# A Griffin-style residual block: eight instead of six of the eleven inner tiles of the last projection as block products

## The chip, the cores and the metric

The kernel runs on one core of a Trainium2 chip. The metric is the device time of one execution in microseconds (us); three runs of the kernel before gave a median of 869.18 us (869.02 to 870.11). The engines of the core are called PE (TensorE, matrix products), DVE (VectorE), ACT (ScalarE), POOL (GpSimd) and SP (SyncE, which here only issues transfers). PE writes its sums to PSUM, eight banks of 128 x 512 floats; everything else lies in SBUF.

## The reference

One trunk layer on 512 frames of 1024 features: an RMS norm, one wide projection, banded attention and an RG-LRU branch, a gated merge, and then the part that the change is about:

```python
h = h + (g_a * ya + g_b * yb) @ w_o[l]
hn = rmsnorm(h, norm_ffn_g[l])
gu = hn @ w_ffn_in[l]                       # 1024 x 5632
g, up = jnp.split(gu, 2, axis=-1)
h = h + (jax.nn.silu(g) * up) @ w_ffn_out[l]   # 512 x 2816 times 2816 x 1024
return rmsnorm(h, final_norm_g)
```

All is float32. A product in this kernel is three matmuls: every operand is split into a high part (type fp32r) and a low remainder, and high x high, high x low and low x high are summed (`mm3`, lines 76 to 78). A split is one ACT copy (the high part, line 82) and then one DVE subtraction (the low part, line 83).

## The kernel before, in words

The stages run one after the other: norm and projections with the RG-LRU work; `v` and the product `yb` with the RG-LRU output (at 160 to 234 us of the profile); attention, head by head; the product `ya` with the attention output (432 to 479 us); `po_h` with `w_o`; norm; the wide feed-forward projection; and the last projection (from 753 us). The order of instructions on each engine and the slots of the buffers come from a planner that simulates the kernel. Inside `manual_schedule(engines={PE, DVE})` the order on PE and on DVE is the order of the program text; ACT's and SP's order is still the planner's. A buffer belongs to a tag with a fixed number of slots, and a new tile waits until all users of the tile that held its slot are done.

**The last projection** has 2816 inner rows, eleven inner tiles of 256. The activations of inner tile i are `act2[i]`, 128 x 2 x 512 floats. The output is eight quarters (t, cc), four token tiles of 128 by two column halves of 512; each has a PSUM bank (`quarter`). A *plain tile* of one inner tile on one quarter is 6 matmuls of 512 columns (`plain_tile`), 48 for all eight quarters.

Two inner tiles together form a *unit*, which is multiplied by the Winograd form of Strassen's scheme: the activations of a unit are four blocks a11, a12, a21, a22 (`part_of`; two inner tiles by two token halves), its weights four blocks b11, b12, b21, b22, and seven block products take the place of eight: a11 x b11, a12 x b21, s1 x t1, s2 x t2, s3 x t3, s4 x b22, a22 x t4, where

```
s1 = a21 + a22    s2 = s1 - a11    s3 = a11 - a21    s4 = a12 - s2
```

and t1 to t4 are such sums of the weights. The weight sums are made far earlier by `spill`: four loads of 512 KB, four DVE subtractions of 128 x 1024, four stores to DRAM (`sums_d`). Every block product is 12 matmuls per unit, in one half of the tokens and one column half (`multiply`). All units add up in PSUM, and between products DVE adds a bank's sum to the rows of `h` that need it (`read`, and `add` for the plain sums).

`make(a, b)` prepares a product: for each unit it loads the weight block (`fo_part`, line 928), splits it into `whl` (128 x 1024 on ACT and DVE), then splits the activation block into `x_` (`act_part`, 128 x 512). The slots: seven for the raw loads, ten for `whl`, and **eight for `x_` (tag "act" of pool `op`)**, which the high and low parts of some plain tiles share. `act2`, the sums and the other plain parts share the 13 slots of the tag "act" of pool `acp`.

Before, the inner tiles are `front` 0, 1, 2 (plain), units (3,4), (5,6), (7,8), and `tail` 9, 10 (plain, at the end, token tile by token tile). The sums s1, s2, s3 of all units are made in one block of DVE work, `act_sums`, while the plain tiles run; s4 in `act_last_sum`. In the tail, each token tile is finished as soon as its two quarters are complete: add to `h` (line 969), sum of squares on ACT (line 971), product with the norm's weights (line 972), then `h_norm`: root, reciprocal, scaling, and the stores.

## Time and profile before

| | |
|---|---|
| median of the runs | 869.18 us |
| the profiled execution, its own time | 869.43 us |
| its span in the trace | 867.6 us |
| PE busy | 855.7 us (99%) |
| DVE busy | 593.1 us (68%) |
| ACT busy | 495.0 us (57%) |
| POOL busy | 96.8 us (11%) |
| moved by DMA | 107.38 MB, 124 GB/s on the mean |

The span is the time between the first and the last event of the trace; some 1.8 us of the execution lie outside. A busy PE means that matmuls are in flight; their ends are modelled, so the distance between starts tells more than busy time does. In a row of a timeline the columns are the start in us, the duration, the engine, the line, the operation, the tile written and those read, and the shape; in brackets stands the idle time of the engine before the instruction and what ended it.

### The profile page before, as it was taken

The page shows a single profiled execution, that of the slowest core. Times are in us where ns is not written, and L with a number is a line of the kernel's source. Part 1 is how long each engine was busy: PE and PEld are TensorE (multiplying, and loading weights), DVE is VectorE, ACT ScalarE, POOL GpSimd, SP SyncE. Part 2 cuts the span into 40 slices and gives each one's busy share as a digit, 9 for nine tenths or more (in the row PEclk, how much of TensorE's full clock was granted, in tenths as well). Part 3 has the DMA queues.
Part 4 walks back from the last instruction along what each step waited for, and adds up shares of the span by engine and source line. Part 5 has one row for each costly group of instructions (what it writes and reads, how often), then busy time and mean ns, then how long its engine had stood idle before and what let it go on. Part 6 is the DMA issues. An engine that isn't in the chain of part 4 may idle for free.

```text
span 867.6 us, 12923 instructions
## 1 busy us (share of the span) xinstructions
PE 855.7 (99%) x4938; PEld 750.3 (86%) x4938; DVE 593.1 (68%) x914; ACT 495.0 (57%) x854; POOL 96.8 (11%) x135
## 2 busy tenths in 40 slices
PE   8999999999999999999999999999999999999996
PEld 6977887888888888888888889999999999888885
DVE  5787776676556656566556556888878888498554
ACT  7588687542366656577633365646555555456504
POOL 2022212110112313222200000000000001000001
PEclk9999999999999999999999999999999999999999
DMA  8222324589542213232223721433433333375402
GB/s 271 91 88 90 97 82 129 199 294 363 149 126 68 73 54 105 73 116 68 72 77 120 266 67 32 150 94 102 142 97 98 98 98 120 124 246 167 145 1 97
DMA packets 89934, 107.38 MB, mean 124 GB/s; under 512 B 5904, under 2 KB 71040, under 8 KB 89872
## 3 DMA queue, kind: packets, MB, share of 16 engines
q1 hardware_dynamic: 86192, 98.89, 35.7%
q10 hardware_dynamic: 3680, 7.67, 2.8%
q8 instruction: 39, 0.64, 0.3%
q14 instruction: 23, 0.19, 0.1%
HBM read 98.11 MB, written 8.43 MB: 123 GB/s over the span
## 4 chain that ended last, share of the span: by engine, by line
PE 86%; DVE 5%; ACT 5%; issue 2%; DMA 2%; POOL 0%; SPq 0%; ACTq 0%; POOLq 0%; DVEq 0%
PE po_out L76 4%; PE po_out L78 4%; PE po_out L77 4%; PE p_fg L76 2%; PE o L711 2%; PE p_fu L78 2%; PE p_fg L78 2%; PE p_fu L77 2%; PE p_fg L77 2%; PE p_fu L76 2%; PE pT L691 2%; PE po_ga L76 2%; PE po_ga L78 2%; PE po_ya L76 2%; PE po_h L78 2%
## 5 line engine op out<-in xcount | busy, mean ns | idle before, releaser
L680 POOL TENSOR_SCALAR p<-p,rl 128x128 f32<-128x128 f32 (+1 forms) x64 | 39.6, 637 | 160.6 <-DVE rl L678 160.5
L677 ACT ACTIVATE p<-p,m 128x128 f32<-128x128 f32 (+1 forms) x64 | 35.8, 562 | 13.2 <-DVE m L676 13.2
L917 POOL TENSOR_TENSOR act_lo<-act,act_hi 128x1024 fp32r<-128x1024 f32 x1 | 2.4, 2417 | 298.6 <-ACT act_hi L916 298.6
L83 DVE TENSOR_TENSOR pp<-pT,pp 128x384 fp32r<-128x384 f32 (+1 forms) x48 | 27.8, 596 | 9.8 <-ACT pp L82 9.7
L83 DVE TENSOR_TENSOR whl_qk<-raw_qk,whl_qk 128x1024 fp32r<-128x1024 f32 x16 | 21.5, 1345 | 14.4 <-ACT whl_qk L82 14.4
L76 PE MATMUL po_out<-whl_fo,act_hi 128*128 128x512 f32 (+1 forms) x80 | 30.8, 385 | 0.5 <-ACT c_u L283 0.5
L78 PE MATMUL po_out<-whl_fo,act_lo 128*128 128x512 f32 (+1 forms) x80 | 30.7, 384 | 0.0
L77 PE MATMUL po_out<-whl_fo,act_hi 128*128 128x512 f32 (+1 forms) x80 | 30.7, 384 | 0.0
L676 DVE CUSTOM_DVE_ANT_0 p<-s,bias 128x128 f32<-128x128 f32 (+1 forms) x64 | 29.2, 483 | 1.8 <-PE s L673 1.8
L83 DVE TENSOR_TENSOR whl_fg_s<-s_fg,whl_fg_s 128x1024 fp32r<-128x1024 f32 x20 | 25.6, 1291 | 5.0 <-ACT whl_fg_s L82 5.0
L76 PE MATMUL po_gr<-xnT,whl_gr 128*128 128x512 f32 (+1 forms) x80 | 28.1, 352 | 0.1
L77 PE MATMUL po_xr<-xnT,whl_xr 128*128 128x512 f32 (+1 forms) x80 | 27.9, 354 | 0.0
L77 PE MATMUL po_gr<-xnT,whl_gr 128*128 128x512 f32 (+1 forms) x80 | 27.8, 348 | 0.0
L78 PE MATMUL po_gr<-xnT,whl_gr 128*128 128x512 f32 (+1 forms) x80 | 27.5, 348 | 0.0
L83 DVE TENSOR_TENSOR whl_fu_s<-s_fu,whl_fu_s 128x1024 fp32r<-128x1024 f32 x20 | 24.0, 1222 | 5.2 <-ACT whl_fu_s L82 5.2
L78 PE MATMUL po_xr<-xnT,whl_xr 128*128 128x512 f32 (+1 forms) x80 | 27.3, 346 | 0.0
L76 PE MATMUL po_xr<-xnT,whl_xr 128*128 128x512 f32 (+1 forms) x80 | 26.6, 351 | 0.6 <-ACT xnT L363 0.6
L82 ACT ACTIVATE whl_fg_s<-s_fg 128x1024 fp32r<-128x1024 f32 x20 | 20.9, 1054 | 10.4 <-PE q_fg L78 5.5
L82 ACT ACTIVATE whl_qk<-raw_qk 128x1024 fp32r<-128x1024 f32 x16 | 16.8, 1051 | 16.2 <-PE po_yb L78 8.8
L76 PE MATMUL po_gb<-xnT,whl_gb 128*128 128x512 f32 x64 | 25.2, 393 | 0.3 <-DVE sp_p L455 0.3
L76 PE MATMUL po_ga<-xnT,whl_ga 128*128 128x512 f32 x64 | 25.3, 395 | 0.0
L77 PE MATMUL po_gb<-xnT,whl_gb 128*128 128x512 f32 x64 | 25.3, 395 | 0.0
(387 smaller groups left out, 3188.0 us busy)
## 6 DMA issues: line engine op xcount, KB each, us to landing
raw_fg<-in_w_ffn_in_dram SPq DMA_DIRECT2D x24, 512.0 KB, 4.4
raw_fu<-in_w_ffn_in_dram SPq DMA_DIRECT2D x22, 512.0 KB, 3.7
raw_qk<-in_w_in_dram SPq DMA_DIRECT2D x32, 256.0 KB, 3.2
spill<-in_w_ffn_out_dram SPq DMA_DIRECT2D x12, 512.0 KB, 4.7
sums<-spill SPq DMA_DIRECT2D x12, 512.0 KB, 3.7
raw_t<-sums SPq DMA_DIRECT2D x12, 512.0 KB, 4.5
raw_fo<-in_w_ffn_out_dram SPq DMA_DIRECT2D x10, 512.0 KB, 4.6
raw_b<-in_w_ffn_out_dram SPq DMA_DIRECT2D x9, 512.0 KB, 4.4
```

The source lines that it names most:

```text
L76: pe.matmul(o, sh, mh, start=start, stop=False, skip_group_check=parts)
L77: pe.matmul(o, sh, ml, start=False, stop=False, skip_group_check=parts)
L78: pe.matmul(o, sl, mh, start=False, stop=stop, skip_group_check=parts)
L82: act.activation(hi, src, AF.Copy)
L83: dve.tensor_sub(lo, src, f(hi))
L676: dve.tensor_tensor_reduce(prob[qb][:], scs[qb], bias[:, S - w:S], -1.0, 3e38, ALU.add, ALU.min, nmax[:, qb:qb + 1])
L677: act.activation(prob[qb][:], prob[qb][:], AF.Exp, bias=nmax[:, qb:qb + 1], scale=-1.0, accum_out=lsum[:, qb:qb + 1])
L680: pool.tensor_scalar(prob[qb][:], prob[qb][:], rl[:, qb:qb + 1], 1.0, ALU.mult, ALU.mult)
L691: pe.transpose(pt[:, at * P:(at + 1) * P], prob[qb][:, kb * P:(kb + 1) * P], ident[:])
L711: pe.matmul(po[:, S - n:S], st, pp[i][:, part, lo:lo + n], start=kb == 0 and part == 0, stop=kb == NT - 1 and part == 1)
L917: (pool if i == 0 else dve).tensor_sub(lo[:], o[:], f(hi[:]))
```

## The change

`front` becomes 0, 1, 10, the units are (2,3), (4,5), (6,7), (8,9), and there is no tail: eight inner tiles go through block products, three stay plain, all three ahead. Four things go with it:

- The sums s1 to s4 are made one at a time, each right before the split that needs it (`act_sum`, called in `act_part`), and s2, s3 and s4 in place.
- The weight sums of the fourth unit need a fourth `spill`. Spill 0 stays where it is; spill 1 moves from the first to the third step of `yb`; spills 2 and 3 are now made in `ya`, at steps 0 and 4, in slots that held queries and keys.
- The order of the products changes, and a12 x b21 comes first, onto the plain sums of quarters (0,0) and (1,0).
- The last two products on the second token half go tokens by tokens: all units for one token tile, then all units for the next. The last unit of the last one is cut into two column halves of 256. `finish` takes the place of `h_out`.

```diff
-    front, units, tail = (0, 1, 2), ((3, 4), (5, 6), (7, 8)), (9, 10)
+    front, units = (0, 1, 10), ((2, 3), (4, 5), (6, 7), (8, 9))
...
-    SPILLS = (0, 3)
     for j in range(KT):
...
-        if j in SPILLS:
-            spill(SPILLS.index(j) + 1)
+        if j == 2:
+            spill(1, [(aw2, "pt", 4)] * 4)
...
     for j in range(KT):
+        if j in (0, 4):
+            spill(2 + j // 4, [(aw, "qk", 3), (qkp, "qk", 3)] * 2)
         py = mm_tile(f"po_ya{j}")
...
-        pl, bufs = (op, 8) if i in front[1:] else (acp, 13)
+        pl, bufs = (op, 8) if i == 1 else (acp, 13)
...
     def act_part(name, u):
-        src = sum_of_act[name, u] if name[0] == "s" else part_of(name, u)
+        src = act_sum(name, u) if name[0] == "s" else part_of(name, u)
         o = op.tile([P, 2, 2, 256], F32R, tag="act", bufs=8, name=f"x_{name}{u}")
         split_pair(o, src)
...
+    def act_sum(name, u):
+
+        if name == "s1":
+            if u % 2 == 0:
+                s_tiles.append(acp.tile([P, 2, 2, 256], F32, tag="act", bufs=13, name=f"s_{u}"))
+            o = s_tiles[-1][:, u % 2]
+            dve.tensor_add(o, part_of("a21", u), part_of("a22", u))
+        elif name == "s2":
+            o = s_tiles[u // 2][:, u % 2]
+            dve.tensor_sub(o, o, part_of("a11", u))
...
+    def finish(cc, t, po, eng, i, at, added=False):
+
+        hs = ht[t][:, cc * S + at.start:cc * S + at.stop]
+        if not added:
+            dve.tensor_add(hs, po[:, at], hs)
+        junk = op.tile([P, S], F32, tag="junk", bufs=2, name=f"oj{t}_{i}")
+        act.activation(junk[:, at], hs, AF.Square, accum_out=osq[t][:, i:i + 1])
+        eng.tensor_mul(hs, hs, g_fin[:, cc * S + at.start:cc * S + at.stop])
...
+        for i, before in zip(front, (None, 1, 10)):
+            if before:
+                split_act(before)
+                for cc in range(2):
+                    fo_plain(before, cc)
+            if i == front[-1]:
+                make("a12", "b21")
+                make("a11", "b11")
+            for t, cc in ((2, 0), (3, 0), (0, 1), (1, 1), (2, 1), (3, 1), (0, 0), (1, 0)):
+                plain_tile(i, t, cc, i == 0)
         make("s1", "t1")
-        for t, cc in ((2, 0), (3, 0), (0, 1), (1, 1), (3, 1)):
+        for t, cc in ((2, 0), (3, 0), (0, 1), (1, 1), (2, 1), (3, 1)):
             add(t, cc)
+        multiply("a12", "b21", 0, 0, False)
         make("s2", "t2")
         multiply("a11", "b11", 1, 0, True)
         read(1, 0, (0, 0))
         multiply("s1", "t1", 0, 1, True)
-        make("a12", "b21")
+        make("s4", "b22")
         read(0, 1, (1, 1))
-        for u in every_unit:
-            act_last_sum(u)
         multiply("s2", "t2", 1, 0, False)
         make("s3", "t3")
         read(1, 0, (0, 1))
...
+        multiply("s4", "b22", 0, 1, False)
         make("a22", "t4")
...
+        for t in range(2):
+            finish(0, t, quarter[t, 0], pool, 0, every)
+        multiply("s3", "t3", 1, 0, False, (0,))
+        multiply("s3", "t3", 1, 0, False, (1,))
+        read(1, 0, (1, 1), (0,))
+        for t in range(2):
+            part = out_norm(t, 1)
+            finish(1, t, quarter[t, 1], dve, 1, every)
+            h_norm(t, part, 1)
+        finish(1, 2, None, pool, 0, every, True)
+        multiply("a22", "t4", 1, 0, False, (0,))
+        read(1, 0, (1, 1), (1,))
+        finish(1, 3, None, pool, 0, every, True)
+        most, last = range(len(units) - 1), [len(units) - 1]
+        multiply("a22", "t4", 1, 0, False, (1,), most)
+        for at in (slice(0, CW), slice(CW, S)):
+            multiply("a22", "t4", 1, 0, False, (1,), last, at)
...
```

More of the change, by code (lines that the diff above doesn't have):

```diff
@@ L741, in fo_block, with spill @@
         return rows.rearrange("(k p) e -> p k e", p=P)
-    def spill(u):
-        r = [aw2.tile([P, 2, S], F32, tag="pt", bufs=4, name=f"spill{u}_{n}") for n in range(4)]
+    def spill(u, rooms):
+        r = [pl.tile([P, 2, S], F32, tag=tag, bufs=bufs, name=f"spill{u}_{n}") for n, (pl, tag, bufs) in enumerate(rooms)]
         for n in range(4):
@@ L754, in spill @@
             sp.dma_start(out=sums_d[u][n][:], in_=r[i][:])
-    spill(0)
+    spill(0, [(aw2, "pt", 4)] * 4)
     for t in range(NT):
         v_tile(0, t)
-    SPILLS = (0, 3)
     for j in range(KT):
@@ L963, in block_kernel @@
     osq = [cp.tile([P, 4], F32, name=f"osq{t}") for t in range(NT)]
-    def h_out(cc, t, po, eng, i, at):
-        n = slice(cc * S + at.start, cc * S + at.stop)
-        hs = ht[t][:, n]
-        dve.tensor_add(hs, po[:, 0:at.stop - at.start], hs)
-        junk = op.tile([P, S], F32, tag="junk", bufs=2, name=f"oj{t}_{i}")
-        act.activation(junk[:, 0:at.stop - at.start], hs, AF.Square, accum_out=osq[t][:, i:i + 1])
-        eng.tensor_mul(hs, hs, g_fin[:, n])
     def out_norm(t, parts):
@@ L1014, in part_of @@
         return act2[units[u][tile_]][:, :, half * 256:half * 256 + 256]
-    sum_of_act = {}
     def act_part(name, u):
-        src = sum_of_act[name, u] if name[0] == "s" else part_of(name, u)
+        src = act_sum(name, u) if name[0] == "s" else part_of(name, u)
         o = op.tile([P, 2, 2, 256], F32R, tag="act", bufs=8, name=f"x_{name}{u}")
@@ L1022, in act_part @@
         acts[name, u] = o
-    def act_sums(u):
-        t = acp.tile([P, 2, 2, 256], F32, tag="act", bufs=13, name=f"s12_{u}")
-        s1, s2 = t[:, 0], t[:, 1]
-        a11, a21, a22 = (part_of(n, u) for n in ("a11", "a21", "a22"))
-        dve.tensor_add(s1, a21, a22)
-        dve.tensor_sub(s2, s1, a11)
-        dve.tensor_sub(a21, a11, a21)
-        sum_of_act.update({("s1", u): s1, ("s2", u): s2, ("s3", u): a21})
-    def act_last_sum(u):
-        a12 = part_of("a12", u)
-        dve.tensor_sub(a12, a12, sum_of_act["s2", u])
-        sum_of_act["s4", u] = a12
+    def act_sum(name, u):
[7 more added lines that the diff above has]
+            dve.tensor_sub(o, o, part_of("a11", u))
+        elif name == "s3":
+            o = part_of("a21", u)
+            dve.tensor_sub(o, part_of("a11", u), o)
+        else:
+            o = part_of("a12", u)
+            dve.tensor_sub(o, o, s_tiles[u // 2][:, u % 2])
+        return o
+    s_tiles = []
     of_weights = {"b11": (0, 0), "b21": (1, 0), "b22": (1, 1)}
@@ L1045, in make, with multiply @@
             act_part(a, u)
-    def multiply(a, b, half, cc, start):
-        for u in range(len(units)):
-            for i in range(2):
+    def multiply(a, b, half, cc, start, tokens=range(2), us=None, at=every):
+        for u in us or range(len(units)):
+            for i in tokens:
                 x, w = acts[a, u], parts_w[b, u]
@@ L1052, in multiply @@
                 for k in range(2):
-                    mm3(quarter[2 * half + i, cc][:], x[:, 0, k, tok], x[:, 1, k, tok], w[:, 0, k], w[:, 1, k],
+                    mm3(quarter[2 * half + i, cc][:, at], x[:, 0, k, tok], x[:, 1, k, tok], w[:, 0, k, at], w[:, 1, k, at],
                         start and u == 0 and k == 0, u == len(units) - 1 and k == 1, parts=True)
-    def read(half, cc, into=None):
-        for i in range(2):
-            t, to = 2 * half + i, 2 * (half if into is None else into[0]) + i
-            n = cc if into is None else into[1]
-            hs = ht[to][:, n * S:(n + 1) * S]
-            dve.tensor_add(hs, quarter[t, cc][:], hs)
@@ L1064, in block_kernel, with read @@
-    every_unit = range(len(units))
-    everywhere = [(t, cc) for cc in range(2) for t in range(NT)]
-    with tc.manual_schedule(engines={mybir.EngineType.PE, mybir.EngineType.DVE}):
-        split_act(1)
-        fo_plain(1, 0)
-        fo_plain(1, 1)
-        for t, cc in everywhere:
-            plain_tile(front[0], t, cc, True)
-        split_act(2)
-        fo_plain(2, 0)
-        fo_plain(2, 1)
-        for t, cc in everywhere:
-            plain_tile(front[1], t, cc, False)
-        make("a11", "b11")
-        for u in every_unit:
-            act_sums(u)
-        for t, cc in ((2, 0), (3, 0), (0, 1), (1, 1), (3, 1), (0, 0), (1, 0), (2, 1)):
-            plain_tile(front[2], t, cc, False)
+    def read(half, cc, into, tokens=range(2)):
+        for i in tokens:
+            hs = ht[2 * into[0] + i][:, into[1] * S:(into[1] + 1) * S]
+            dve.tensor_add(hs, quarter[2 * half + i, cc][:], hs)
@@ L1088, in block_kernel @@
         multiply("s1", "t1", 0, 1, True)
-        make("a12", "b21")
+        make("s4", "b22")
         read(0, 1, (1, 1))
-        for u in every_unit:
-            act_last_sum(u)
         multiply("s2", "t2", 1, 0, False)
@@ L1095, in block_kernel @@
         read(1, 0, (0, 1))
-        multiply("a12", "b21", 0, 0, False)
-        make("s4", "b22")
-        multiply("s3", "t3", 1, 0, False)
-        read(1, 0, (1, 1))
+        multiply("s4", "b22", 0, 1, False)
         make("a22", "t4")
-        multiply("s4", "b22", 0, 1, False)
-        for i in tail:
-            split_act(i)
-            for cc in range(2):
-                fo_plain(i, cc)
-        multiply("a22", "t4", 1, 0, False)
-        for t in range(NT):
-            for i in tail:
-                plain_tile(i, t, 0, False)
-            h_out(0, t, quarter[t, 0], pool, 0, every)
-            pieces = [(quarter[t, 1], every, False)]
-            if t == NT - 1:
-                last = mm_tile("po_last")
-                pieces = [(quarter[t, 1], slice(0, CW), True), (last, slice(CW, S), True)]
-            for n, (po, at, start) in enumerate(pieces):
-                for i in tail:
-                    plain_tile(i, t, 1, start and i == tail[0], at, po[:, 0:at.stop - at.start])
-                if n == len(pieces) - 1:
-                    part = out_norm(t, n + 1)
-                h_out(1, t, po, dve, n + 1, at)
-            h_norm(t, part, n + 1)
+        for t in range(2):
[15 more added lines that the diff above has]
+            multiply("a22", "t4", 1, 0, False, (1,), last, at)
+        part = out_norm(2, 1)
+        finish(0, 2, quarter[2, 0], dve, 1, every)
+        h_norm(2, part, 1)
+        finish(0, 3, quarter[3, 0], dve, 1, slice(0, CW))
+        part = out_norm(3, 2)
+        finish(0, 3, quarter[3, 0], dve, 2, slice(CW, S))
+        h_norm(3, part, 2)
 _INS = ["x", "norm_mix_g", "w_in", "b_merge", "rel_table", "w_attn_out", "conv_w", "conv_b", "w_rg_r", "b_rg_r",
```

## The prediction

> **What bounds the kernel now.** I read the page's engine line first, then PE's waits, then the busy time by stage.

> ```profile
> span 867.6 us, 12923 instructions
> PE 855.7 (99%) x4938; PEld 750.3 (86%) x4938; DVE 593.1 (68%) x914; ACT 495.0 (57%) x854; POOL 96.8 (11%) x135
> ...
> PE po_out L76 <- ACT c_u L283: 0.5, 1, 0.5
> ...
> PE po_v L76 <- DVE v L83: 0.3, 1, 0.3
> ...
> 753.00:782.00 29.00, 28.81 (x127) 23.85 (x128) 27.05 (x33) 18.40 (x23) 0.00 (x0) 1.00 0.73 251
> 782.00:839.00 57.00, 57.00 (x253) 47.20 (x252) 40.39 (x48) 25.62 (x32) 0.00 (x0) 1.00 0.36 113
> 839.00:861.00 22.00, 22.00 (x109) 18.59 (x107) 9.79 (x21) 9.60 (x23) 4.99 (x4) 1.00 0.19 72
> ```

> The last three rows are the last projection: plain tiles, products, tail. Their columns are the stretch, busy time (and count) of PE, weight load, DVE, ACT and POOL, the granted clock, DMA share and GB/s. PE waits there once, 0.5 us. DVE is busy 40.4 of 57 us beside the products and 9.8 of 22 in the tail: it follows PE with room, and the change spends that room.

> ```profile
> 753.19 0.50 PE L76 MATMUL po_out<-whl_fo,act_hi 128*128 128x512 f32 x1 [0.47 <-ACT c_u L283]
> ...
> 830.86 0.39 PE L76 MATMUL po_out<-whl_t,x_a 128*128 128x512 f32 x1
> ...
> 838.79 0.39 PE L78 MATMUL po_out<-whl_t,x_a 128*128 128x512 f32 x1
> ...
> 859.37 0.28 PE L78 MATMUL po_out<-whl_fo,act_lo 128*128 128x256 f32 x1
> ...
> 859.49 0.28 PE L76 MATMUL po_last<-whl_fo,act_hi 128*128 128x256 f32 x1
> ...
> 859.69 0.42 DVE L969 TENSOR_TENSOR h<-po_out,h 128x256 f32<-128x256 f32 x1 [0.65 <-PE po_out L78]
> ...
> 860.81 0.28 PE L78 MATMUL po_last<-whl_fo,act_lo 128*128 128x256 f32 x1
> ```

> The 36 matmuls of a22 x t4 start from 830.86 to 838.79: 7.93 / 35 = 0.2266 us each. So 6 of them (a unit on one token tile, or a plain tile on a quarter) take 1.36 us, a unit in a product 2.72, a product of four units 10.88. The twelve half-width ones from 859.49 to 860.81 stand 0.12 apart; PE is through at 860.93.

> **PE's work.** Before, 5 x 48 + 3 x 7 x 12 = 492 matmuls, twelve of them cut into 24 halves: 480 x 0.2266 + 24 x 0.12 = 111.65 us. After, 3 x 48 + 4 x 7 x 12 = 480, six of them cut into twelve halves: 474 x 0.2266 + 12 x 0.12 = 108.85. **PE saves 2.8 us.**

> **DVE's work in a product.** Rows of DVE and ACT while s1 and t1 are prepared:

> ```profile
> 768.29 0.69 DVE L1028 TENSOR_TENSOR s<-act,act 128x512 f32<-128x512 f32 x1
> ...
> 769.01 0.63 ACT L82 ACTIVATE x_s<-s 128x512 fp32r<-128x512 f32 x1 [0.28 <-DVE s L1028]
> ...
> 774.08 1.22 DVE L83 TENSOR_TENSOR whl_t<-raw_t,whl_t 128x1024 fp32r<-128x1024 f32 x1
> 775.22 0.69 DVE L83 TENSOR_TENSOR x_s<-s,x_s 128x512 fp32r<-128x512 f32 x1
> 775.82 1.22 DVE L83 TENSOR_TENSOR whl_t<-raw_t,whl_t 128x1024 fp32r<-128x1024 f32 x1
> ```

> Back to back, DVE needs 1.14 us for a unit's weights and 0.60 for its `x_`: 1.74. In the new order the sum comes between them, and `x_` needs ACT's copy of that very sum: 1.14 + sum 0.69 + 0.04 + ACT 0.63 + 0.04 + 0.60 = **3.14 us per unit** (0.04 is the hand-over: 768.29 + 0.69 to 769.01). Four units make 12.56, and two `read` adds 1.2 more: 13.76 us of DVE for each of s1, s2, s4, s3, against 10.88 of PE. Before, the sums were made ahead and DVE never stood between them and the split. So DVE becomes the bound, if it has no lead.

> **Its lead is cut by the slots.** `x_` has eight slots. These rows show such slots at work before: the copy waits for the PE product that last used its slot, and one `x_` follows the other at 2.72 us, PE's time for a unit.

> ```profile
> 787.54 0.63 ACT L82 ACTIVATE x_a<-act 128x512 fp32r<-128x512 f32 x1 [1.14 <-PE po_out L78]
> ...
> 790.26 0.63 ACT L82 ACTIVATE x_a<-act 128x512 fp32r<-128x512 f32 x1 [1.14 <-PE po_out L78]
> ...
> 821.54 0.69 DVE L1062 TENSOR_TENSOR h<-po_out,h 128x512 f32<-128x512 f32 x1 [9.00 <-PE po_out L78]
> ```

> The third row is the other half of it: DVE stood 9 us at a `read`, in program order, with later work behind it. After the change, a12 and a11 of four units fill all eight slots. `x_` of s1, unit u, waits until PE is through with a12, unit u. In DVE's text the six `add`s stand behind all of s1, and PE's next product a11 x b11 overwrites quarters (2,0), (3,0), so it waits for the first `add`. Queued there: a11 on PE, and behind the adds all of s2.

> The chain, with PE never late until then: 753.19 + 126 plain matmuls (18 of 144 ran earlier, inside the feed-forward) x 0.2266 = 781.75, a12 begins. Unit 0 is done at 784.5, drained 0.16 later (0.39 - 0.23); ACT and DVE make s1's first `x_` by 785.95. Three more units at 3.14: 795.4. First add 0.69: **a11 starts at 796.1; PE was free at 792.6, so it stalls 3.5 us.** All adds end at 799.0; s2 and reads 812.8; s4 and reads 826.5; s3 839.1 and the first read 839.8. PE could start s3 x t3 at 796.1 + 43.5 = 839.6: stall 0.2. Second read 840.3, a22 (4 x 1.74) 847.3, two finishing adds 1.2, the first read of s3 0.6: 849.1. Then DVE finishes tokens 0 and 1 ahead of the read that a22's second token tile needs. Their prices in the tail of before:

> ```profile
> 844.66 0.69 DVE L969 TENSOR_TENSOR h<-po_out,h 128x512 f32<-128x512 f32 x1 [1.08 <-PE po_out L78]
> ...
> 846.13 1.28 ACT L986 ACT_TABLE_LOAD   x1
> ...
> 848.49 0.68 DVE L969 TENSOR_TENSOR h<-po_out,h 128x512 f32<-128x512 f32 x1
> ...
> 850.10 0.69 DVE L969 TENSOR_TENSOR h<-po_out,h 128x512 f32<-128x512 f32 x1
> ...
> 852.92 0.69 DVE L969 TENSOR_TENSOR h<-po_out,h 128x512 f32<-128x512 f32 x1
> ```

> 3.83 us for the first (844.66 to 848.49, with ACT's table load of 1.28) and 2.82 for the second (850.10 to 852.92): 855.75, the read 0.7: 856.5. PE has a22's first token tiles done at 839.8 + 16.3 = 856.1: stall 0.4. Then 18 matmuls and 12 halves, 5.5 us: PE ends at 862.0, **1.1 later than before**, though it has 2.8 less to do.

> **The end.** Before, the half that ends at 859.37 + 0.12 = 859.49 starts the last chain (add 859.69, square, product, add of the other half), 8.1 us to the end of the span; twelve half matmuls hide behind it. After, six do, so the first half is ready only 0.72 before PE's end where it was 1.44: **+0.7.** The sum so far is +1.8.

> **ACT in the way.** The 3.14 hold when ACT is free at the moment the sum is done, 16 times. ACT also copies the weights, 1.05 us each, in an order that the planner sets:

> ```profile
> L82 ACT ACTIVATE whl_t<-raw_t 128x1024 fp32r<-128x1024 f32 x12 | 12.3, 1048 | 8.1 <-issue 6.5 <-PE po_out L78 1.6
> ```

> No such meeting is to be seen before, since DVE had a lead. Bounds: 0, and a full copy in every second case, 8 x 1.05 = 8.4. I take chance (1.05 of 3.14, a third) times half a copy, 16 x 0.17 = 2.7, since nothing ties ACT's order to DVE's. All of it lies on the chain. **Sum: +4.5.**

> **The moved spills.** Four loads, four subtractions (about 1.2 us each like the other 128x1024 rows), four stores, on SP ahead of `ya`'s and `w_o`'s weight loads.

> ```profile
> 160.00:195.00 35.00, 34.70 (x156) 28.57 (x155) 24.07 (x31) 14.41 (x24) 6.47 (x4) 1.00 0.88 298
> ...
> 432.00:479.00 47.00, 47.00 (x211) 38.99 (x211) 28.94 (x36) 17.36 (x22) 0.00 (x0) 1.00 0.36 114
> ```

> `ya` has 18 us of free DVE for 10 us of subtractions, and two thirds of the DMA time for 8.4 MB. In the first row, where a spill and more shared the queue, PE lost 0.3 us. I take +0.3 here; bounds -0.3 (yb is relieved) and +2 (SP held at a store while `w_o` waits). The order of plain tiles changes which bank is first, so the 0.47 us ahead of 753.19 may go or double: 0, bounds +-0.5. `a22`'s and `s3`'s token-by-token order costs nothing: by then the chain on DVE, above, is late anyway. Tokens 2 and 3 have a product with the norm's weights on POOL, with products of PE ahead of its use.

> [...]

> ```profile
> 861.00:862.00 1.00, 0.09 (x1) 0.00 (x0) 0.97 (x4) 0.00 (x0) 0.18 (x1) 1.00 0.00 0
> ...
> 864.00:865.00 1.00, 0.00 (x0) 0.00 (x0) 0.00 (x0) 0.00 (x0) 0.00 (x0) 0.58 0.29 118
> ...
> 1.18 5.01 PE L309 MATMUL busy<-idle 128*128 128x512 bf16 x16 [1.18 <-DVE eps_t L315]
> ```

> PE ends at 861.09, and the granted clock falls to a half at 864.16 (0.58 is the mean of 0.16 at 1.00 and 0.84 at 0.50), 3.1 us later; a stall of 3.5 reaches that. The nearest price of a slow start is the 16 matmuls at the kernel's start, 5.01 us where 16 x 0.2266 are 3.63: 1.4. PE would then come to s3 at 841.0 and DVE at 839.8, and a22's wait would vanish: end 862.8 for 862.0 without ACT's waits, and nothing with them, since DVE then stays later than PE. [...]

> **Rivals.**
> - *PE still sets the time* (chance 0.13): the adds come through before PE needs them and ACT serves each sum at once, so only -2.8 + 0.7 = -2.1 remain: 867.3. For it: PE 99% busy, DVE with 17 us of room in the products before. Against: the count of eight slots and the text order leave s1's last `x_` no earlier than a12's end.
> - *DVE late, but little* (0.10): the stall at a11 is its minimum, 0.16 + 0.63 + 0.69 + 0.69 = 2.2, since DVE caught up on unit 3, and later stalls vanish: -2.8 + 2.2 + 0.7 = +0.1, 869.5. Against: 3.14 per unit is slower than the slots come free (2.72).
> - *SP blocks in `ya`* (0.05): a store waits for DVE, `w_o` behind it; one such hold, 4 subtractions of 1.2 us, +5 on whatever else holds, 879.
> - *The sums are not late in fact* (within the second): if s1 were ready before 781.75, ACT would still wait for the slot; the cycle would be 1.74 and the time that of the second rival.

> **How the numbers follow.** The profiled run took 869.43 us, 0.25 above the median. 869.43 + 4.5 + 0.3 = 874.2, against the median 873.9; this is the likeliest case (0.72). Its own range: without ACT's waits and spill 871.0; with 3 us more of ACT's waits and 1 of the spill 878. 0.2% is 1.7 us, about what a measurement of this kernel can tell from no change. Faster 0.13 (first rival), within 0.10 (second), slower 0.77. The range 869.4 to 878 leaves out the first rival and the far end of the third.

> **What would show it.** Right: a PE wait of 3 to 5 us for an `add`, at the first matmul of a11 x b11 some 39 us into the stage; DVE busy or waiting for ACT's `x_s` from there to s3; PE's matmuls 12 fewer; smaller waits at s3 and at a22's second token tile; the end 0.7 longer behind PE. Wrong: no PE wait at a11 (slots or order are not as I count), DVE's cycle far from 3.14, or idle PE in `ya` or `po_h`.

## The result, and the profile after

The changed kernel takes **884.66 us** (median, 883.74 to 885.75) where the kernel before takes 869.1 beside it: a ratio of 1.0177, with a 95% interval of 1.016 to 1.0195. That is 15.5 us slower. The forecast was 873.9, in a range of 869.4 to 878.0: the direction held, the size was three times too small. The profiled execution took 885.43 us, with a span of 883.6, which is 16.0 more than before.

The page of the changed kernel, its head, and from the list of costliest groups POOL's normalization of the attention's probabilities (busy time, then mean ns of one):

```profile
span 883.6 us, 12951 instructions
...
PE 859.6 (97%) x4920; PEld 751.1 (85%) x4920; DVE 605.9 (69%) x929; ACT 501.0 (57%) x862; POOL 102.1 (12%) x135
...
L680 POOL TENSOR_SCALAR p<-p,rl 128x128 f32<-128x128 f32 (+1 forms) x64 | 43.9, 703 | 163.8 <-DVE rl L678 163.7
```

PE has 18 matmuls less, and it waits more. Its waits, with the total, how often, and the longest:

```profile
PE pT L691 <- POOL p L680: 4.8, 4, 2.1
...
PE po_out L76 <- DVE h L999: 3.9, 1, 3.9
PE po_out L76 <- DVE h L1056: 1.7, 1, 1.7
...
PE po_out L76 <- DVE part L973: 0.9, 1, 0.9
PE po_out L77 <- DVE whl_fo L83: 0.8, 1, 0.8
```

The forecast named the second, third and fourth (line numbers of the changed kernel: 999 is the `add`, 1056 the `read`, 973 the norm of a token tile). It did not name the first, and that one is not in the last projection at all: line 680 normalizes the probabilities of an attention head, line 691 transposes them.

**Where the 16 us are.** PE's first plain product starts at 744.13 in the kernel before and at 751.58 after: 7.45 us are lost before the last projection begins. PE ends at 861.09 before and at 876.24 after: another 7.7 are lost inside it. The end of the span is 6.51 behind PE before, 7.36 after: the last 0.85.

**The attention's part.** Twenty microseconds around the last head. Columns as in the tables by stage: stretch, busy time (and count) of PE, weight load, DVE, ACT, POOL, granted clock, DMA share, GB/s. First the kernel before, then the changed one with stretches of 1 us below it:

```profile
420.00:440.00 20.00, 20.00 (x100) 16.96 (x99) 8.28 (x14) 8.07 (x16) 2.05 (x4) 1.00 0.20 60
```

```profile
420.00:440.00 20.00, 15.19 (x63) 12.21 (x62) 11.11 (x15) 6.15 (x12) 6.30 (x4) 0.83 0.74 263
...
427.00:428.00 1.00, 0.29 (x1) 0.14 (x1) 1.00 (x3) 0.00 (x0) 1.00 (x2) 0.92 0.98 389
428.00:429.00 1.00, 0.10 (x1) 0.00 (x0) 1.00 (x1) 0.00 (x0) 1.00 (x1) 0.50 1.20 272
...
434.00:435.00 1.00, 1.00 (x5) 0.83 (x4) 0.00 (x0) 0.00 (x0) 0.00 (x0) 0.67 0.79 313
```

POOL's four normalizations of the last head take 6.30 us instead of 2.05, PE stands idle for 4.8, and then the granted clock is at a half until some time in the stretch from 434. What stands beside POOL is DVE with the weight sums of the moved spills (lines 749 to 752), and the four normalizations apart show when it hurts. Rows of the changed kernel's timeline, then its groups of POOL by shape, then those of the kernel before:

```profile
422.46 1.22 DVE L749 TENSOR_TENSOR spill<-spill,spill 128x1024 f32<-128x1024 f32 x1 [0.91 <-DMA spill<-in_w_ffn_out_dram]
423.60 0.17 DVE L678 RECIPROCAL rl<-l 128x4 f32<-128x4 f32 x1
423.72 1.22 DVE L750 TENSOR_TENSOR spill<-spill,spill 128x1024 f32<-128x1024 f32 x1
...
426.18 1.21 DVE L749 TENSOR_TENSOR spill<-spill,spill 128x1024 f32<-128x1024 f32 x1
...
427.91 1.21 DVE L752 TENSOR_TENSOR spill<-spill,spill 128x1024 f32<-128x1024 f32 x1
```

```profile
L680 POOL TENSOR_SCALAR p<-p,rl 128x256 f32<-128x256 f32 x1 | 2.5, 2488 | 0.0
L680 POOL TENSOR_SCALAR p<-p,rl 128x384 f32<-128x384 f32 x1 | 1.9, 1942 | 0.0
L680 POOL TENSOR_SCALAR p<-p,rl 128x128 f32<-128x128 f32 x1 | 1.2, 1242 | 8.9 <-DVE rl L678 8.9
L680 POOL TENSOR_SCALAR p<-p,rl 128x512 f32<-128x512 f32 x1 | 0.7, 685 | 0.0
```

```profile
L680 POOL TENSOR_SCALAR p<-p,rl 128x512 f32<-128x512 f32 x1 | 0.7, 692 | 0.0
L680 POOL TENSOR_SCALAR p<-p,rl 128x384 f32<-128x384 f32 x1 | 0.6, 586 | 0.0
L680 POOL TENSOR_SCALAR p<-p,rl 128x256 f32<-128x256 f32 x1 | 0.5, 480 | 0.0
L680 POOL TENSOR_SCALAR p<-p,rl 128x128 f32<-128x128 f32 x1 | 0.4, 372 | 7.2 <-DVE rl L678 7.2
```

The three normalizations that run beside DVE's row of subtractions take three to five times as long; the last and largest, behind the row, takes its usual 0.69. Added up from POOL's start at 423.94, the three end at 425.18, 427.67 and 429.61, each within half a microsecond after the end of a subtraction (424.94, 427.39, 429.12). Two more things are in the first of these three fences. The subtractions are not where the text has them, in `ya`: outside the stretches that are written out by hand the planner orders DVE, and it pulled them forward into the last head. And the reciprocal that POOL needs stands behind a subtraction that itself waits 0.91 us for a load.

**The last projection's part.** PE at a11 x b11, then the clock of the stretches around it:

```profile
805.05 0.77 PE L76 MATMUL po_out<-whl_b,x_a 128*128 128x512 f32 x1 [3.95 <-DVE h L999]
...
810.23 0.39 PE L76 MATMUL po_out<-whl_b,x_a 128*128 128x512 f32 x1
```

```profile
803.00:804.00 1.00, 0.00 (x0) 0.00 (x0) 0.38 (x1) 0.58 (x1) 0.00 (x0) 0.65 0.56 78
804.00:805.00 1.00, 0.00 (x0) 0.00 (x0) 1.00 (x3) 0.00 (x0) 0.00 (x0) 0.50 0.99 379
...
810.00:811.00 1.00, 1.00 (x6) 0.85 (x5) 0.00 (x0) 0.57 (x2) 0.00 (x0) 0.94 0.73 201
```

PE stalls 3.95 us for the first `add` and then runs twelve matmuls in 5.18 us where they need 2.72. DVE in the same stage, where the number in brackets is how long it stood for ACT's copy of the sum that it had just made, and one row of ACT, at 834.96:

```profile
793.65 0.69 DVE L83 TENSOR_TENSOR x_s<-s,x_s 128x512 fp32r<-128x512 f32 x1 [3.18 <-ACT x_s L82]
...
797.37 0.69 DVE L83 TENSOR_TENSOR x_s<-s,x_s 128x512 fp32r<-128x512 f32 x1 [1.29 <-ACT x_s L82]
...
800.49 0.69 DVE L83 TENSOR_TENSOR x_s<-s,x_s 128x512 fp32r<-128x512 f32 x1 [0.70 <-ACT x_s L82]
...
803.62 0.69 DVE L83 TENSOR_TENSOR x_s<-s,x_s 128x512 fp32r<-128x512 f32 x1 [0.70 <-ACT x_s L82]
804.23 3.67 DVE L999 TENSOR_TENSOR h<-po_out,h 128x512 f32<-128x512 f32 x6
...
834.96 1.06 ACT L82 ACTIVATE whl_t<-raw_t 128x1024 fp32r<-128x1024 f32 x1 [1.71 <-PE po_out L78]
...
836.57 0.69 DVE L83 TENSOR_TENSOR x_s<-act,x_s 128x512 fp32r<-128x512 f32 x1 [1.91 <-ACT x_s L82]
...
842.01 0.69 DVE L83 TENSOR_TENSOR x_s<-act,x_s 128x512 fp32r<-128x512 f32 x1 [1.82 <-ACT x_s L82]
...
852.06 1.28 DVE L1056 TENSOR_TENSOR h<-po_out,h 128x512 f32<-128x512 f32 x2
...
865.47 0.55 DVE L982 TENSOR_SCALAR h<-h,ors 128x640 f32<-128x640 f32 x1
...
868.54 1.23 DVE L982 TENSOR_SCALAR h<-h,ors 128x640 f32<-128x640 f32 x1
...
876.28 0.42 DVE L1062 TENSOR_TENSOR h<-po_out,h 128x256 f32<-128x256 f32 x1 [2.50 <-PE po_out L78]
```

800.49 to 803.62 is the cycle of one unit, 3.13 us, and the six adds stand behind the last split of s1, as forecast. Where a weight copy stood ahead of the sum's copy on ACT the cycle is longer. In the longest waits, 1.91 and 1.82 us, that weight copy was itself held up. In the first of the two the sum was ready at 834.66, but ACT stood until 834.96 for the weights' slot, which PE had still in use, and then copied the weights first.

### The profile page after: what moved, and what is told of

It reads as the page before. It is cut to its first block, busy times and chain, and to the rows that moved or that the text cites. A ratio compares the mean times of both kernels' runs of the same rounds, so it can differ in the third digit from the quotient of the medians.

```text
span 883.6 us, 12951 instructions
## 1 busy us (share of the span) xinstructions
PE 859.6 (97%) x4920; PEld 751.1 (85%) x4920; DVE 605.9 (69%) x929; ACT 501.0 (57%) x862; POOL 102.1 (12%) x135
## 4 chain that ended last, share of the span: by engine, by line
PE 91%; DVE 4%; ACT 3%; DMA 1%; issue 1%; POOL 1%; SPq 0%; DVEq 0%; ACTq 0%; POOLq 0%
PE po_out L76 3%; PE po_out L77 3%; PE po_out L78 3%; PE p_fg L76 2%; PE p_fu L78 2%; PE p_fg L78 2%; PE p_fg L77 2%; PE p_fu L77 2%; PE p_fu L76 2%; PE pT L691 2%; PE o L711 2%; PE po_gb L77 2%; PE po_gb L76 2%; PE po_v L76 2%; PE po_q L76 2%; PE po_ya L78 2%
## 5 line engine op out<-in xcount | busy, mean ns | idle before, releaser
L680 POOL TENSOR_SCALAR p<-p,rl 128x128 f32<-128x128 f32 (+1 forms) x64 | 43.9, 703 | 163.8 <-DVE rl L678 163.7
L83 DVE TENSOR_TENSOR pp<-pT,pp 128x384 fp32r<-128x384 f32 (+1 forms) x48 | 27.9, 596 | 12.6 <-ACT pp L82 12.5
L83 DVE TENSOR_TENSOR whl_qk<-raw_qk,whl_qk 128x1024 fp32r<-128x1024 f32 x16 | 21.5, 1345 | 14.4 <-ACT whl_qk L82 14.4
L83 DVE TENSOR_TENSOR whl_fg_s<-s_fg,whl_fg_s 128x1024 fp32r<-128x1024 f32 x20 | 25.5, 1290 | 5.0 <-ACT whl_fg_s L82 5.0
L76 PE MATMUL po_gr<-xnT,whl_gr 128*128 128x512 f32 (+1 forms) x80 | 28.1, 352 | 0.1
L78 PE MATMUL po_gr<-xnT,whl_gr 128*128 128x512 f32 (+1 forms) x80 | 27.5, 348 | 0.0
L83 DVE TENSOR_TENSOR whl_fu_s<-s_fu,whl_fu_s 128x1024 fp32r<-128x1024 f32 x20 | 24.0, 1220 | 5.2 <-ACT whl_fu_s L82 5.2
L82 ACT ACTIVATE whl_t<-raw_t 128x1024 fp32r<-128x1024 f32 x16 | 17.0, 1060 | 18.4 <-PE po_out L78 12.6
L78 PE MATMUL po_xr<-xnT,whl_xr 128*128 128x512 f32 (+1 forms) x80 | 27.3, 346 | 0.0
L76 PE MATMUL po_xr<-xnT,whl_xr 128*128 128x512 f32 (+1 forms) x80 | 26.6, 351 | 0.6 <-ACT xnT L363 0.6
L82 ACT ACTIVATE whl_fg_s<-s_fg 128x1024 fp32r<-128x1024 f32 x20 | 20.9, 1054 | 10.4 <-PE q_fg L78 5.5
L691 PE MATMUL pT<-ident,p 128*128 128x128 f32 x160 | 21.9, 282 | 4.8 <-POOL p L680 4.8
L82 ACT ACTIVATE pp<-pT 128x384 fp32r<-128x384 f32 (+1 forms) x48 | 22.0, 528 | 7.0 <-PE pT L691 6.7
L76 PE MATMUL po_ga<-xnT,whl_ga 128*128 128x512 f32 x64 | 26.0, 405 | 0.0
L82 ACT ACTIVATE whl_qk<-raw_qk 128x1024 fp32r<-128x1024 f32 x16 | 16.8, 1051 | 15.9 <-PE po_yb L78 8.8
L76 PE MATMUL po_gb<-xnT,whl_gb 128*128 128x512 f32 x64 | 25.2, 393 | 0.3 <-DVE sp_p L455 0.3
L78 PE MATMUL po_ga<-xnT,whl_ga 128*128 128x512 f32 x64 | 25.5, 398 | 0.0
```

The lines of the kernel that those rows point to most:

```text
L76: pe.matmul(o, sh, mh, start=start, stop=False, skip_group_check=parts)
L78: pe.matmul(o, sl, mh, start=False, stop=stop, skip_group_check=parts)
L82: act.activation(hi, src, AF.Copy)
L83: dve.tensor_sub(lo, src, f(hi))
L680: pool.tensor_scalar(prob[qb][:], prob[qb][:], rl[:, qb:qb + 1], 1.0, ALU.mult, ALU.mult)
L691: pe.transpose(pt[:, at * P:(at + 1) * P], prob[qb][:, kb * P:(kb + 1) * P], ident[:])
```

## The experiments

Two losses, two theories. **A**: in attention, DVE's subtractions slow POOL, PE waits, and the clock falls behind the wait. **C**: in the last projection, DVE's order (sums between the splits, adds behind s1) makes DVE the bound. The first runs take each on its own.

### The spills' places alone, in the kernel before

```diff
...
-    SPILLS = (0, 3)
     for j in range(KT):
...
-        if j in SPILLS:
-            spill(SPILLS.index(j) + 1)
+        if j == 2:
+            spill(1, [(aw2, "pt", 4)] * 4)
...
     for j in range(KT):
+        if j in (0, 4):
+            spill(2 + j // 4, [(aw, "qk", 3), (qkp, "qk", 3)] * 2)
```

> The kernel before, its last projection as it was, with the spills placed as the change places them: one in yb, two at ya (the fourth, of units 9 and 10, is stored and never read). In the trace of the changed kernel the last attention head took 7.9 us longer: POOL's four normalizations of the probabilities took 6.30 us where they took 2.05, beside DVE's subtractions of the spills, PE waited 4.8 us for them and the clock then fell to a half. Theory A (the moved subtractions slow POOL in the last head): 869.1 + 7.9 = 877, with the same POOL row near 6 us and PE waits of some 4.8 us for p. Rival B (the spills' transfers, not DVE's work, crowd it): 877 too, told apart by the run without subtractions. Rival R (the plan of the order of work shifted for another reason, tied to the new last projection): 869, with POOL at 2 us.

Measured: **877.06 us** (876.86 to 877.24), ratio 1.0089 with an interval of 1.0074 to 1.0104. The same 7.9 us, with the last projection as it was:

```profile
420.00:440.00 20.00, 15.33 (x61) 12.26 (x60) 11.14 (x15) 5.78 (x12) 6.30 (x4) 0.83 0.72 261
```

Rival R falls. The spills are the cause of the attention's loss, by DVE or by their transfers.

### The change with its late spills in yb

```diff
-        if j == 2:
-            spill(1, [(aw2, "pt", 4)] * 4)
+        if j in (0, 2, 4):
+            spill(1 + j // 2, [(aw2, "pt", 4)] * 4)
...
-        if j in (0, 4):
-            spill(2 + j // 4, [(aw, "qk", 3), (qkp, "qk", 3)] * 2)
```

> The changed kernel with its three late spills at yb j = 0, 2 and 4, none at ya. Theory A (the spills' subtractions slow POOL in the last head): the 7.9 us go, 884.7 - 7.9 = 876.8, give or take 0.5 for a spill more in yb; the last projection keeps its stalls. Rival Y (yb, where DMA is 0.88 busy already, loses as much to a third spill): 882 to 885, with PE waits in yb instead. Rival R (not the spills): 884.7, POOL's four still at 6 us.

Measured: **878.05 us** (877.24 to 879.99), ratio 1.0103 (1.0088 to 1.0118). In the last head POOL's four take 2.06 us again and PE does not wait for them. The span is 876.4, 7.2 less than the change's; `yb` takes three spills without a new wait of PE. On the medians 6.6 us are gained, where 7.9 were expected. A holds, Y and R fall. The slowing has not gone, it has moved. A spill now stands beside the first head, whose four take 2.06 us in the kernel before:

```profile
226.88 3.82 POOL L680 TENSOR_SCALAR p<-p,rl 128x128 f32<-128x128 f32 x4 [50.78 <-DVE rl L678]
```

It costs nothing there: PE has products of `yb` to do and comes to that head's transposes at 233.35, when the normalizations are long done.

### DVE or the transfers: the last head on ACT, and the spills without subtractions

```diff
-            pool.tensor_scalar(prob[qb][:], prob[qb][:], rl[:, qb:qb + 1], 1.0, ALU.mult, ALU.mult)
+            if h == HEADS - 1:
+                act.activation(prob[qb][:], prob[qb][:], AF.Copy, scale=rl[:, qb:qb + 1])
+            else:
+                pool.tensor_scalar(prob[qb][:], prob[qb][:], rl[:, qb:qb + 1], 1.0, ALU.mult, ALU.mult)
```

> The changed kernel, spills left in place, with the normalization of the last head's probabilities on ACT instead of POOL. Theory A (POOL is slowed by DVE's subtractions beside it): ACT is not slowed, PE's 4.8 us of waits for p and the half clock behind them go, 877 to 878. Rival B (transfers crowd whatever works there) or D (DVE itself is late with the reciprocal, since the subtractions stand ahead of it): PE waits as long for ACT, 883 to 885.

```diff
-        dve.tensor_sub(b11, b12, b11)
-        dve.tensor_sub(b12, b22, b12)
-        dve.tensor_sub(b22, b22, b11)
-        dve.tensor_sub(b21, b21, b22)
+        if u < 2:
+            dve.tensor_sub(b11, b12, b11)
+            dve.tensor_sub(b12, b22, b12)
+            dve.tensor_sub(b22, b22, b11)
+            dve.tensor_sub(b21, b21, b22)
```

> The changed kernel without the four subtractions in each of the two spills at ya: their loads and stores stay in place, and the sums of weights of units 2 and 3 are left out of the computation. Theory A (DVE's subtractions slow POOL): POOL's four at some 2 us, no PE wait for p, 877. Rival B (the spills' transfers crowd POOL or PE's operands): POOL's four at 6 us, 884.7.

Measured: **878.32 us** with the last head on ACT (878.01 to 879.36; ratio 1.0106, 1.0089 to 1.0123), and **877.80** in a single run without the subtractions. Waits of the first, and the last head's stretch of the second:

```profile
PE pT L694 <- ACT p L681: 0.5, 2, 0.3
```

```profile
420.00:440.00 20.00, 20.00 (x100) 16.97 (x99) 8.75 (x16) 8.54 (x17) 2.06 (x4) 1.00 0.81 279
```

The second row decides against rival B: DMA is busier (0.81) than in the change (0.74), and PE is busy all the time, POOL at 2.06. On ACT, with every subtraction and transfer in place, 0.5 us of waiting is left. The reciprocal stands behind a subtraction in that run too (which waits 0.58 us for its load, 0.91 in the change), so D, the late reciprocal, is worth about as much. The two runs gain 6.3 and 6.9 of the 7.9 us: nearly all of it needs POOL and DVE's subtractions side by side.

What the two engines share, the rows do not show. What is added to one normalization, 1242 - 372 = 0.87, 1942 - 586 = 1.36 and 2488 - 480 = 2.0 us, is between 0.7 and 1.7 subtractions of 1.2 us, and each slowed normalization ends 0.24 to 0.49 us after a subtraction does.

### One input instead of two

The subtractions left out as before, and in their place:

```diff
...
+        else:
+            for b in (b11, b12, b22, b21):
+                dve.tensor_scalar(b, b, 0.5, None, ALU.mult)
```

> The changed kernel with each subtraction of the two spills at ya replaced by a product with a constant, one input and the same tile as output: the transfers and their order stay, the sums of weights of units 2 and 3 are left out of the computation. If POOL is slowed by any DVE work over SBUF beside it: its four normalizations at 4 to 6 us, PE waits for p of 2 to 5 us, 881 to 885. If only by instructions with two inputs from SBUF: 2 to 3 us, no wait, 877 to 878 as without the subtractions.

Measured: **881.13 us** in a single run. The time and PE's waits, 2.1 us, are at the edge of what was expected for any DVE work, POOL's four in the last head at that for two inputs only. DVE in that head:

```profile
424.70 0.69 DVE L756 TENSOR_SCALAR spill<-spill 128x1024 f32<-128x1024 f32 x1 [2.09 <-DMA spill<-in_w_ffn_out_dram]
425.31 0.17 DVE L678 RECIPROCAL rl<-l 128x4 f32<-128x4 f32 x1
426.01 0.70 DVE L756 TENSOR_SCALAR spill<-spill 128x1024 f32<-128x1024 f32 x1 [0.54 <-DMA spill<-in_w_ffn_out_dram]
427.36 0.72 DVE L756 TENSOR_SCALAR spill<-spill 128x1024 f32<-128x1024 f32 x1 [0.65 <-DMA spill<-in_w_ffn_out_dram]
```

POOL's four take 3.00 us, 0.95 more than with no spill beside them. The first three of them take 1.9 us, from 425.64 to the start of the fourth at 427.5, where they take 1.44 in the kernel before, and all that DVE starts meanwhile is two such products, at 426.01 and 427.36. So instructions with one input slow POOL too; they are also shorter (0.69 instead of 1.22) and there are fewer of them beside it. The first of the two spills was moved further ahead in this run, into another head, at 399.47: there POOL's four take 5.70 us, 3.02 in the kernel before, with one-input products and two-input splits of DVE side by side, and PE does not wait. PE's 2.1 us of waits have a second source as well: in the last head the reciprocal stands behind an instruction that waits 2.09 us for its load. The run does not tell how much the number of inputs matters, nor how much of the waits is POOL's and how much the late reciprocal's.

### The adds first

```diff
-        make("s1", "t1")
         for t, cc in ((2, 0), (3, 0), (0, 1), (1, 1), (2, 1), (3, 1)):
             add(t, cc)
+        make("s1", "t1")
```

> The changed kernel with the six adds put ahead of s1's and t1's preparation in DVE's order; nothing else. Theory C (a11 waits because the adds stand behind s1, whose last split waits for a12's slot): the wait of 3.9 us at a11 and the 2.5 us of half clock behind it go; DVE's cycle of 3.13 us per unit stays, and it becomes late at a later product: DVE's chain ends as before or a little earlier, PE is late at s1 or s3 by some 2 to 6 us instead. Total 880 to 883. Rival E (the stall at a11 is all that the last projection loses, DVE has room behind it): 884.7 - 6.4 = 878.3. Rival F (the adds are late because of their own wait for PE, not of their place): 884.7.

Measured: **886.74 us** (886.33 to 887.83), ratio 1.0202 (1.0187 to 1.0217), some 2 us *slower* than the change. Its waits and, in the two stretches where they lie, the clock:

```profile
PE po_out L76 <- DVE h L1056: 7.2, 2, 4.1
```

```profile
830.00:840.00 10.00, 6.87 (x25) 5.33 (x24) 6.36 (x10) 3.90 (x5) 0.00 (x0) 0.84 0.38 113
...
850.00:860.00 10.00, 6.27 (x21) 5.05 (x22) 9.24 (x12) 2.71 (x5) 0.00 (x0) 0.83 0.00 0
```

The wait at a11 is gone, and 7.2 us stand at two later products, each followed by a spell at half clock. E and F fall. DVE's chain comes to s3's first read at 852.90 where it came there at 852.06: moving the adds shortened nothing, since DVE has the same work in a row, and ACT's weight copies were more in the way this time: behind s1 the three longest waits for `x_s` are 3.53, 2.20 and 2.13 us, in the change 1.91, 1.82 and 1.46. The stall that was taken from one place on a late engine came back at the next. The forecast of 880 to 883 was too low by the copies and the second spell.

### The sums ahead of the splits

```diff
...
     def make(a, b):
+        srcs = [act_sum(a, u) if a[0] == "s" else None for u in range(len(units))]
         for u in range(len(units)):
...
-            act_part(a, u)
+            act_part(a, u, srcs[u])
```

> The changed kernel with the sums of a product's four units made in a row ahead of its splits; spills and adds where the change has them. Theory C (the sum between weight split and input split puts ACT's copy on DVE's chain: 3.13 us per unit where PE takes 2.72): DVE's need is 0.65 + 1.74 = 2.4 us per unit, less than PE's; the stall at a11 falls to its least, drain 0.16 + copy 0.63 + split 0.69 + add 0.69 = 2.2, too short for the clock to fall, and the waits at s3 (1.7) and a22 (0.9) go: 884.7 - 1.8 - 2.5 - 1.7 - 0.9 = 877.8. Rival G (DVE has too much to do, whatever the order of its work): at most 1 us is gained, 883.7 to 884.7. Rival H (ACT's weight copies in the planner's order are what is late): the waits for x_s stay, 881 to 883.

Measured: **879.37 us** (877.57 to 879.93), ratio 1.0114 (1.01 to 1.0128). The waits at s3 and a22 are gone, the one at a11 is down to its least, 2.1. G and H fall. But the clock fell all the same. That it would not at this length was the author's estimate; no run had shown it:

```profile
803.04 0.51 PE L76 MATMUL po_out<-whl_b,x_a 128*128 128x512 f32 x1 [2.14 <-DVE h L999]
803.35 0.63 PE L77 MATMUL po_out<-whl_b,x_a 128*128 128x512 f32 x1
...
806.76 0.40 PE L76 MATMUL po_out<-whl_b,x_a 128*128 128x512 f32 x1
```

Nine matmuls take 3.72 us instead of 2.04. That 1.7 is about the difference from the 877.8 expected.

### All three, and what was left

The spills in `yb`, the adds first and the sums ahead, together:

> The changed kernel with three edits: late spills at yb j = 0, 2, 4, adds ahead of s1, sums of four units ahead of the splits. If the three causes (spills beside POOL, adds behind s1, sums inside the chain) are all that the change lost: PE's 2.8 us saved less 0.7 at the end and 0.8 more of waiting for the second front tile's weights, less 0.5 of the wait for c_u that is gone: 869.2 - 2.8 + 0.7 + 0.8 - 0.5 = 867.4, and no PE wait over 1 us in the last projection. If a wait is left that none of them explains: 869 to 873.

Measured: **868.39 us** (867.82 to 870.18), ratio 0.9992 (0.9983 to 1.0001): 16.3 us less than the change, and no difference from the kernel before that can be told. It is 1.0 more than the 867.4 expected. No wait of PE over 1 us is left in the last projection. Together the three edits take back the whole loss. Alone, the adds in front gained nothing and the sums ahead gained 5; no run has the adds behind s1 with the other two edits in place, so what the adds' place is worth beside them is not measured. The longest of POOL's normalizations takes 2.71 us here, 1.55 in the kernel before, and again none of PE's waits is for them. Of the last projection's stalls nothing remains but this:

```profile
PE po_out L77 <- DVE whl_fo L83: 0.8, 1, 0.8
```

Two more edits, a front tile's weights asked for one tile earlier and twelve half matmuls instead of six behind the first half of the last token tile:

```diff
-        for i, before in zip(front, (None, 1, 10)):
-            if before:
-                split_act(before)
+        for i, ahead in zip(front, (1, 10, None)):
+            if ahead:
+                split_act(ahead)
...
-        most, last = range(len(units) - 1), [len(units) - 1]
+        most, last = range(len(units) - 2), range(len(units) - 2, len(units))
```

> The kernel with the three edits (spills in yb, adds ahead of s1, sums ahead of the splits) and two more: the splits and weights of a front tile are asked for one tile earlier, ahead of the plain products of the tile before it; and the last token tile's halves take the last two units instead of one (twelve half products behind the first half, as in the kernel before). If the wait of 0.8 for the second front tile's weights comes from ACT taking six x_a copies ahead of them, and the tail's 0.7 from too few half products: 868.4 - 0.8 - 0.7 = 866.9, with no PE wait for whl_fo and the first half ready 1.4 before PE's end. Rival: ACT's order is the planner's and the wait stays, 867.7; or the last chain is bound by the second half anyway, 867.6; neither helps, 868.4.

Measured: **868.45 us** (867.93 to 869.52), ratio 0.9996 (0.9987 to 1.0005). Neither helped. The wait of 0.8 is still there: on ACT six copies `x_a`, 3.2 us in a row, stand ahead of the front tile's weights, in an order that is the planner's. And the first half's add still waits for PE's very last matmul, at 858.94 with PE through at 858.90, as at 876.28 in the changed kernel, since both halves lie in one tile of PSUM. So the last two runs take these two causes themselves away.

```diff
-    with tc.manual_schedule(engines={mybir.EngineType.PE, mybir.EngineType.DVE}):
+    with tc.manual_schedule(engines={mybir.EngineType.PE, mybir.EngineType.DVE, mybir.EngineType.Activation}):
```

> The kernel with the three edits (spills in yb, adds ahead of s1, sums ahead of the splits), with ACT's work of the last projection in the order of the text too, as PE's and DVE's is; nothing else. The wait of 0.8 for the second front tile's weights stayed when they were asked for a tile earlier, with six x_a copies (3.2 us) ahead of them on ACT. If that order is its cause, the copies now come behind the front tiles' weights: no PE wait for whl_fo, 868.4 - 0.8 = 867.6. If the wait is the weights' transfer, it stays: 868.4. If ACT in text order is late for DVE (a unit's weights behind the unit before's input): PE waits in the products, 869 to 872.

Measured: **866.74 us** (866.56 to 867.25), ratio **0.9973** (0.9963 to 0.9983). The wait is gone. The gain of 1.65 on the medians is twice the 0.8 expected; in the profiles 0.7 of it is a wait that varies at the kernel's start (`pt_mix`, 1.7 and 1.0).

```diff
...
+        multiply("a22", "t4", 1, 0, False, (1,), last, slice(0, CW))
+        po_last = mm_tile("po_last")
...
-        finish(0, 3, quarter[3, 0], dve, 1, slice(0, CW))
+        dve.tensor_add(ht[3][:, 0:S], quarter[3, 0][:], ht[3][:, 0:S])
+        finish(0, 3, None, dve, 1, slice(0, CW), True)
         part = out_norm(3, 2)
-        finish(0, 3, quarter[3, 0], dve, 2, slice(CW, S))
+        dve.tensor_add(ht[3][:, CW:S], po_last[:, 0:S - CW], ht[3][:, CW:S])
+        finish(0, 3, None, dve, 2, slice(CW, S), True)
```

> As the kernel with ACT in text order, and for the last token tile the second half of the columns of the last two units goes to a tile of its own in PSUM (added to h on its own), as in the kernel before; the first half's columns then end twelve half products before PE does. In the kernels with one tile for both halves the first half's add waited for PE's very last product (876.28 in the changed kernel, PE through at 876.24), so the end stood 7.4 us behind PE where it stood 6.5 before. If the common tile is the cause: the first half's add starts 1.2 to 1.4 before PE's end, the end stands 6.5 behind PE, and the time is 0.7 to 0.9 less than with ACT's order alone: 866.8. If the add of the whole width and one more add eat it: 867.6.

Measured: **866.60 us** (865.49 to 867.03), ratio **0.997** (0.9957 to 0.9982).

```profile
856.88 0.69 DVE L1117 TENSOR_TENSOR h<-po_out,h 128x512 f32<-128x512 f32 x1 [1.19 <-PE po_out L78]
...
858.00 0.28 PE L78 MATMUL po_last<-whl_t,x_a 128*128 128x256 f32 x1
```

The first half's add now starts 1.4 us before PE is through (858.28), and the end of the span, 864.5, is 6.2 behind PE instead of 7.4. The common tile was the cause of the late add. In the time the 0.7 to 0.9 expected do not show: the medians are 0.14 apart, which these runs cannot tell from nothing. PE was through 1.1 later in this profile, and 0.96 of it is there at the first plain product already (744.71 against 743.75): the wait at the start is 2.0 here where it was 1.0, and the mean granted clock of the profile 0.996 where it was 0.999. Both kernels are some 2.4 us faster than the kernel before.

## Why the prediction was wrong in size

**The step that failed: "I take +0.3 here; bounds -0.3 (yb is relieved) and +2".** That is the term of the moved spills. It measured 7.9 alone (877.06 against 869.19) and 7.45 in the changed kernel. With 7.45 in its place the forecast would have been 881, three quarters of the way. Its working compared free DVE time and free DMA time in `ya`, and asked who waits on SP. Two things were not asked: whether the work stays in `ya`, since the planner orders DVE there and moved it into the last head; and what DVE's work does to a neighbour that is not waiting for it. The kernel before shows the latter. Line 680 of two heads, one after the other:

```profile
412.48 3.02 POOL L680 TENSOR_SCALAR p<-p,rl 128x128 f32<-128x128 f32 x4 [7.33 <-DVE rl L678]
422.71 2.05 POOL L680 TENSOR_SCALAR p<-p,rl 128x128 f32<-128x128 f32 x4 [7.21 <-DVE rl L678]
```

The same four instructions take 2.05 or 3.02 us, and this row was not read.

**The last projection, by the forecast's own times**, up to PE's end, which it put at 862.0 without ACT's waits and which came at 876.24, 14.2 later:

| stretch | forecast | measured | difference |
|---|---|---|---|
| first plain product, shift | 0 | 744.13 to 751.58 | 7.45 |
| a12's start, beyond that shift | 781.75 | 790.06 | 0.86 |
| a12's start to a11's start | 14.35 | 14.99 | 0.64 |
| a11's start to s3's | 43.7 | 47.84 | 4.14 |
| s3's start to a22's second token tile | 16.7 | 17.53 | 0.83 |
| from there to PE's end | 5.5 | 5.82 | 0.32 |

(In the last row 0.16 is a matter of counting: the forecast took PE to be through 0.12 after the start of its last matmul, 876.24 is the modelled end.)

- *The slots and the order* were right: a12 to a11 14.99 instead of 14.35, the stall 3.95 instead of 3.5, at the product that was named, for the `add` that was named. *DVE's cycle*: 3.13 measured for 3.14.
- *ACT in the way*, 2.7 taken, bounds 0 and 8.4: a unit waits 0.70 at the least (0.63 and two hand-overs); beyond that DVE stood 0.59 before a11 and 4.33 behind it, together 4.9, of the right kind and inside the bounds, but 2.2 more than taken. It is nearly all of the 0.64 and the 4.14. Not all of it is ACT's: at 811.10 the copy waited for its slot behind PE's slow twelve matmuls, 0.76 of the 4.9. And 1.21 and 1.12 of it, at 836.57 and 842.01, are not the chance meeting with a running copy that was priced: a weight copy that waited for PE stood ahead in ACT's order. That the size came out within a factor of two is luck in part.
- *Not in the forecast*: the second front tile's weights, behind ACT's `x_a` copies, a PE wait of 0.76 at 771.12 with some slow steps around it. The 0.86 are what this cost less the 0.47 ahead of 753.19, which the forecast kept and which is gone; "The order of plain tiles ... 0, bounds +-0.5" had looked at the bank only.
- *The tokens' finishing* took 0.83 longer, by the second of its two: 866.00 to 869.69, 3.69 instead of 2.82 (the first, from 862.07 to 866.00, 3.93 instead of 3.83). In it DVE's scaling at 868.54 takes 1.23 where the same shape takes 0.55 at 865.47, while POOL works on a product with the norm's weights from 868.13 to 869.42. Here POOL slows DVE, by the look of the rows; no run took it apart.
- *The tail*, +0.7: measured 7.36 - 6.51 = 0.85, but the reason was wrong. The first half is not ready 0.72 before PE's end; its add waits for the last matmul, since the halves share a tile. The number came out near by chance.
- *The clock*: "nothing with them, since DVE then stays later than PE". In the change the half clock at a11 costs PE 5.18 - 2.72 = 2.46 us, and PE still waits 1.7 at s3 for DVE; but for the 0.76 that comes back through the slot it is absorbed, as said. In attention nothing absorbs it, and there it is part of the 7.9. The row's price of 1.4 was too low: one spell cost 1.7 with the sums ahead (3.72 - 2.04), the double one at a11 2.46. And its 3.1 us from PE's end to the fall do not measure the idle time that a fall takes: a stall of 2.14 us was enough, and in the changed kernel the fall came 2.2 us after PE's end (878.40 after 876.24).
- *Two of its signs* do not follow from its own working. "PE's matmuls 12 fewer" counts two half-width matmuls as one: 504 - 486 = 18, as measured. And "some 39 us into the stage" is where PE was to be free (792.6); a11 was to start at 796.1, 43 us in.
- *The rivals*: PE did not set the time; DVE was not late but little; SP did not block. The third rival's place, the spills in `ya`, was near, its mechanism was another.

## What to carry to other kernels

Work that is moved into a stage with room on its own engine has to be held against the neighbours of that engine too: look up how long the same instructions of POOL take when DVE is busy beside them and when it is not, and where the planner is free to put the moved work. Then ask who waits for that neighbour: POOL beside a spill cost 7.9 us in the last head and nothing in the first. On an engine that is late, only a shorter chain helps; taking a wait from one product moved it to the next. Make sums that feed another engine's copy for all units in a row, so that the copy runs while the next sum is made.
